# The last features of the second feed-forward product: as plain products in the slabs' seven banks instead of eight output tiles

## The chip, the core and the metric

The kernel runs on one core of a Trainium2 chip. It is one program for the whole two-layer trunk, launched once. The metric is device time in microseconds (us) of one execution, as the median of several runs; one more execution was recorded by the profiler, and everything that is said below about single instructions comes from that execution.

## The reference, cut to what matters

The trunk works on 256 tokens of width 2048 in float32. Layer 0 has a pooling mixer and memory attention, layer 1 differential and memory attention; each ends in the same feed-forward part:

```python
D_MODEL, SEQ, DEPTH, D_FF = 2048, 256, 2, 8192

def squared_relu_mlp(h, w1, w2):
    z = jax.nn.relu(h @ w1)
    return (z * z) @ w2

def reference(...):
    for i in range(DEPTH):
        ...                                   # attention or pooling, output projection
        x = x + squared_relu_mlp(rms_norm(x, ffn_norm[i]), w_ff1[i], w_ff2[i])
    return x
```

The change is in `(z * z) @ w2`, 8192 features to 2048 columns, in both layers. After layer 0's comes the projection of the shared keys and values; layer 1's is the last thing that the program does.

## The kernel before, in words

**Precision.** A float32 product is made of three passes in a rounded float32 format. Both factors are split into a high part (a cast) and a low part (value minus high part): for activations once, beforehand; for weights as they stream in. A weight goes from memory into `raw` (or `slab`, `room`), ScalarE casts it into a slot of `hi_ring` (line 195), and VectorE subtracts for `lo_ring` (line 198). The rings have six slots of 512 columns. `Feed.fill` prepares weights three jobs ahead of the job that TensorE is on (`AHEAD`), and not before slots are free. The load of a weight itself is issued further ahead, from SyncE.

**Tiles.** In a tile (`a_part`, lines 456 and 458) the weight block of 128 x 128 is the stationary side. A matmul against high and low part of the activations (512 columns) and one against the high part alone (256 columns) give 128 output columns for all tokens, transposed, as the residual `resid` is held. `c_tile` (lines 470 to 472) does the same in three matmuls of 256 columns.

**Slabs.** For most of the second product the weights are the moving side. A slab takes a pair of 128-feature blocks (256 features), both token halves, and two 512-column groups (one half `g` of the 2048 columns), as a 2 x 2 block product in the form with seven products in place of eight. Each of the seven has its own PSUM bank, p0 to p6, in which all slabs of the half add up. A product is three matmuls of 128 x 512 (`product`, lines 943, 945, 946). The seven are done as four jobs, with weights that are sums of the four weight blocks:

- job 0, the left blocks as loaded (1024 columns in `slab`), banks 0 and 1;
- job 1, the first 512 columns of `slab`, after a DMA from POOL (GpSimd) has added another weight block in place (`add_right`, line 170, issued after job 0's split), bank 2;
- job 2, the second weight row (`room`, 1024 columns), after VectorE added job 1's sum to it (line 224), banks 3 and 4;
- job 3, `room` again, after a second POOL DMA has added a block to it (issued after job 2's split) and VectorE one more (line 238), banks 6 and 5.

So within a slab there are four splits and two POOL DMAs in one chain. The jobs of neighbouring slabs overlap: slab p's jobs 1 and 2 come between job 0 of slab p+1 and job 3 of slab p-1.

**Order of the work.** Python code writes the instructions down in order; `at(n, ...)` puts a step n ticks later, `tick()` passes one. A scheduler then orders each engine's queue by its estimates. The 56 first-product tiles of a layer (`up_tile`) produce 64 blocks of features; 8 of these blocks come from a block product of the same kind ahead of them. A table of due times (`tiles_at`) spreads slab jobs between the tiles. The slabs of the halves alternate in groups of four pairs; at a change of half `swap` copies each bank out and `restore` (line 1093) copies the other half's back.

**The end of the product before.** Half 0 gets all 32 pairs as slabs, half 1 only the first 24, so there are 56 slabs. For the last 8 pairs (16 blocks of features), half 1's 1024 columns are done as eight tiles of 16 blocks, `down_tile(0)` to `down_tile(7)`. Twelve slab jobs of half 0 are left when they begin, two before each of tiles 0 to 5, and `finish_banks` closes half 0 within the last tiles: it adds up the banks (lines 1170 to 1174), scales rows, turns 128 x 128 pieces on TensorE (`turn`, line 1185) and adds them to `resid` (line 1186). Half 1's banks were closed earlier (`close_left`, `turn_left`, line 1146). In layer 1 tile 7 is a `c_tile`, over 12 blocks of `z` and then over 4 in `zr` that were scaled beforehand (line 901), so that after the last matmul one addition (line 915) and one output DMA (line 2049) remain. `done(n)` sends output column block n in layer 1, and prepares the next norm in layer 0.

Of the kernel before, what the change touches and what calls it, by code (L numbers as in the profile page):

```python
# [17 lines left out]
P = 128  # L18
# [8 lines left out]
PER_PART = 56  # L27
# [28 lines left out]
class Plan:  # L56
# [7 lines left out]
    def __init__(self):  # L64
        self.entries = []
        self.npos = 0
        self.jobs = []
        self.slabs = []

# [31 lines left out]
class Feed:  # L101
# [65 lines left out]
    def add_right(self, n, t):  # L167

        h = self.plan.row["S", n, 1]
        self.nc.gpsimd.dma_start(t, self.wst[h, :, 0:512], accum_op=ALU.add)  # L170
# [40 lines left out]
    def _prepare(self, p):  # L211
# [22 lines left out]
        if p[2] == 0:  # L234
            self.add_right(p[1], ra[:, 0:512])
        elif p[2] == 2:
            self.add_right(p[1], rb[:, 512:1024])
            add(rb[:, 0:512], rb[:, 0:512], ra[:, 512:1024])
# [35 lines left out]

    def used(self, n=1):
# [6 lines left out]
    def slab(self, rows):  # L282

        if self.dry:
            self.plan.slabs.append(rows)
        self.slab_no += 1
        return self.slab_no - 1
# [9 lines left out]
    def job_used(self, n, j):  # L297
        if not self.dry:
            self.free(("S", n, j))

# [11 lines left out]
def program(ctx, tc, plan, dry, xT, memT, par, lam, cst, wst, yT):  # L312
# [129 lines left out]
    def a_part(ps, w, l, n, ks, xs, first=True, last=True, between=None, rows=None):  # L442
# [4 lines left out]
        while i < len(ks):  # L447
# [7 lines left out]
            for c, k, hi, lo in two:  # L455
                nc.tensor.matmul(ps, hi, xs[:, k, :], start=first and c == 0, stop=False)  # L456
# [337 lines left out]
    def ffn(l, xs, tags, done, z, sums_in, f_place):  # L794
# [6 lines left out]

        room = sp.tile([P, 8192], F32, tag=tags[1], name=f"room{l}")
        staged = sp.tile([P, 2048], F32, tag="big2", name=f"stage{l}")
        sit = [sums_in[:, j, :] for j in range(4)]
        stage = [staged[:, T * j : T * j + T] for j in range(6)]
        sums = [room[:, 512 * j : 512 * j + 512] for j in range(2)]
        outs = [room[:, 1024 + 512 * j : 1536 + 512 * j] for j in range(2)]
# [19 lines left out]
        def evict(ps):  # L827
            x = outs[cnt[0] % 2]
            cnt[0] += 1
            return x, nc.scalar.copy(x, ps)  # L830
# [4 lines left out]
        def convert(j):  # L835
            a = stage[j % 6]
            k = j % NK

            def high():
                z_free[k] = False  # L840
                nc.scalar.copy(z[:, k, 0:T], a)
                at(1, low)

            def low():
                nc.vector.tensor_sub(z[:, k, T : 2 * T], a, z[:, k, 0:T].bitcast(F32))
# [3 lines left out]
            if j % 2 == 0:  # L849
                return  # L850
            i = j // 2

            def ready():
                return j in z_done and j - 1 in z_done and sit_free[i % 4]

            def combine():
                summed_up.add(i)
                sit_free[i % 4] = False
                a11, a21 = stage[2 * i % 6][:, 0:P], stage[2 * i % 6][:, P:T]
                a12, a22 = stage[(2 * i + 1) % 6][:, 0:P], stage[(2 * i + 1) % 6][:, P:T]  # L860
                s1, s2, s3, s4 = (sums[i % 2][:, c * P : c * P + P] for c in range(4))
                nc.vector.tensor_sub(s1, a21, a22)
                nc.vector.tensor_sub(s3, a11, a21)
                nc.vector.tensor_sub(s2, s1, a11)
                nc.vector.tensor_add(s4, a12, s2)
                at(1, sums_high)
                at(2, sums_low)

            def sums_high():
                nc.scalar.copy(sit[i % 4][:, 0:512], sums[i % 2])  # L870

            def sums_low():
                nc.vector.tensor_sub(
                    sit[i % 4][:, 512:1024], sums[i % 2], sit[i % 4][:, 0:512].bitcast(F32)
                )
                sit_done.add(i)

            when(ready, combine)

        def up_tile(i, ps, between=None):  # L880
# [5 lines left out]
            y, out = evict(ps)  # L886
            at(1, lambda: nc.vector.tensor_add(y[:, 0:T], y[:, 0:T], y[:, T : 2 * T]))
            at(2, lambda: nc.scalar.activation(y[:, 0:T], y[:, 0:T], AF.Relu))

            def square():  # L890
                assert i < 6 or i - 6 in z_done and (i - 6) // 2 in summed_up
                nc.scalar.activation(stage[i % 6], y[:, 0:T], AF.Square)
                at(1, lambda: convert(i))

            at(2, square, 2)

        scaled = []

        def scale_z(j):
            a, b = stage[j % 6], scaled[0][:, j % NK, :]  # L900
            one = nc.vector.tensor_mul(a, a, r[0])
            if not dry:
                feed.order(one, feed.last_cast.ins.name)
            split_plain(b, a)

        def down_tile(n, ps, between=None):
            ks = range(3 * NK, 4 * NK)
            if l == 1 and n == 7:
                c_tile(ps, "w_ff2", l, n, ks[:12], z, feat)
                x = outs[cnt[0] % 2]  # L910
                nc.vector.tensor_mul(x[:, 0:T], ps[:, 0:T], r[0])
                nc.vector.tensor_add(resid[:, n, :], resid[:, n, :], x[:, 0:T])
                ps = mmt("ff2")
                c_tile(ps, "w_ff2", l, n, ks[12:], scaled[0], feat)
                nc.vector.tensor_add(resid[:, n, :], resid[:, n, :], ps[:, 0:T])
                done(n)
                return
            if l == 1 and n == 6:
                scaled.append(sp.tile([P, NK, 512], F32R, tag="S0", name="zr"))
                for j in ks[12:]:  # L920
                    at(j - 59, lambda j=j: scale_z(j))
            a_part(ps, "w_ff2", l, n, ks, z, between=between, rows=feat)
            x, _ = evict(ps)

            def add():
                nc.vector.tensor_add(x[:, 0:T], x[:, 0:T], x[:, T : 2 * T])
                nc.vector.tensor_mul(x[:, 0:T], x[:, 0:T], r[0])
                nc.vector.tensor_add(resid[:, n, :], resid[:, n, :], x[:, 0:T])
                done(n)

            at(1, add)
# [16 lines left out]
        def slab_jobs(g, i, again, end):  # L948
# [4 lines left out]
                    [("w_ff2", l, feat[k], c, 4), ("w_ff2", l, feat[k + 1], c, 4)]  # L953
# [4 lines left out]
            def plain(c, t):  # L958
                assert k + c in z_done
                zk = z[:, (k + c) % NK, :]  # L960
                return zk[:, t * P : t * P + P], zk[:, T + t * P : T + t * P + P]
# [13 lines left out]
            def run(j):  # L975
                hi, lo = feed.job(n, j)
                for c, (p, a) in enumerate(sides[j]):
                    s = slice(512 * c, 512 * c + 512)
                    assert holds[p] == g
                    product(p, g, end, a(), hi[:, s], lo[:, s])  # L980
                feed.job_used(n, j)
                if j == 3 and not again:
                    sit_free[i % 4] = True
                    if i < 24:
                        z_free[k % NK] = z_free[(k + 1) % NK] = True

            return run

# [45 lines left out]
        def close_first(j):  # L1034
# [20 lines left out]
            for p in of_job[j]:  # L1055
                restore(p, 0)

        def turn_first(h):
# [7 lines left out]
            x, _ = evict(t4.rearrange("p c t -> p (c t)"))  # L1066
# [3 lines left out]

            def square():
                for k in (i, i + 1):
                    assert k < 6 or k - 6 in z_done and (k - 6) // 2 in summed_up
                nc.scalar.activation(staged[:, T * (i % 6) : T * (i % 6) + 512], x, AF.Square)
                at(1, lambda: convert(i))
# [1058 lines left out]
```

## Time and profile before

| | |
|---|---|
| median of 3 runs | 1983.58 us (1983.49 to 1983.89) |
| profiled execution: its span | 1982.8 us |
| TensorE (PE) busy | 1977.6 us |
| VectorE (DVE) busy | 1806.6 us |
| ScalarE (ACT) busy | 1571.6 us |
| GpSimd (POOL) busy | 239.3 us |
| layer 0's eight tiles end at | about 913 us |
| layer 1's last 56 tiles, slabs and eight tiles end at | about 1979 us |

The profiled execution has no time of its own beside its span: its span is 0.8 us under the median of the timed runs. In a row of the trace a time "907.88 0.62" is a start and a duration in us. A TensorE duration contains its pipeline's depth, so the rate is read from the starts of consecutive matmuls. In a row by shape, "x192 | 60.2, 395 | 0.0" means 192 instructions, 60.2 us busy, 395 ns each on average, and 0.0 us of idle time just before them. "PEld" is the load of the stationary side, SP is SyncE, and "SPq" and "POOLq" are the queues through which these engines issue DMAs.

### The profile page before, as it was taken

What the parts mean: (1) busy time and instruction counts of PE and PEld (TensorE: products, weight loads), DVE (VectorE), ACT (ScalarE), POOL (GpSimd) and SP (SyncE); (2) the same over time, 40 slices, a digit from 0 to 9 for tenths busy, and PEclk for the clock granted to TensorE, in tenths of its full rate; (3) what the DMA queues carried; (4) which work ended last, traced back from release to release, by engine and by line L of the source; (5) the groups of instructions that cost most, each with busy time, mean ns of one, the idle gap of its engine ahead of it and who ended that gap; (6) DMA issues with size and microseconds to landing.
All of it is one profiled execution on the core that took longest, in us unless ns stands there. A gap on an engine that the chain in (4) does not pass through costs nothing.

```text
span 1982.8 us, 31946 instructions
## 1 busy us (share of the span) xinstructions
PE 1977.6 (100%) x10356; PEld 1685.5 (85%) x10356; DVE 1806.6 (91%) x3313; ACT 1571.6 (79%) x2886; POOL 239.3 (12%) x281
## 2 busy tenths in 40 slices
PE   9999999999999999999999999999999999999999
PEld 7888888888888888888888889888888888888888
DVE  8898889999999999889989798989999999999888
ACT  7766677788878888778768799777788888888775
POOL 0000011111111111110110000001111111111110
PEclk9999999999999999999999999999999999999999
DMA  9556578888888888767886434568888888988874
GB/s 312 183 183 195 189 207 229 236 232 235 237 233 232 231 233 227 226 182 222 246 222 191 166 127 143 197 188 240 235 231 229 235 234 229 242 231 227 227 207 146
DMA packets 151080, 426.92 MB, mean 215 GB/s; under 512 B 17024, under 2 KB 19712, under 8 KB 150912
## 3 DMA queue, kind: packets, MB, share of 16 engines
q1 hardware_dynamic: 111024, 352.50, 53.2%
q0 software_dynamic: 39744, 72.37, 22.0%
q8 instruction: 81, 1.33, 0.3%
q14 instruction: 87, 0.71, 0.1%
q10 hardware_dynamic: 144, 0.01, 0.0%
HBM read 422.72 MB, written 2.10 MB: 214 GB/s over the span
## 4 chain that ended last, share of the span: by engine, by line
PE 99%; DMA 0%; ACT 0%; SPq 0%; issue 0%; DVE 0%; ACTq 0%
PE x_bank L456 22%; PE x_bank L458 11%; PE p L943 10%; PE p L945 10%; PE p L946 10%; PE wo L456 6%; PE wo L458 3%; PE u L456 2%; PE ff L456 1%; PE u L458 1%; PE q L490 1%; PE q L492 1%; PE q L491 1%; PE mk L492 1%; PE mk L490 1%; PE vp L1642 1%
## 5 line engine op out<-in xcount | busy, mean ns | idle before, releaser
L195 ACT CAST hi_ring<-raw 128x512 fp32r<-128x512 f32 x897 | 547.5, 620 | 167.3 <-PE x_bank L456 39.7
L198 DVE TENSOR_TENSOR lo_ring<-raw,hi_ring 128x512 fp32r<-128x512 f32 x897 | 605.1, 686 | 46.7 <-ACT hi_ring L195 39.9
L456 PE MATMUL x_bank<-fx,hi_ring 128*128 128x512 f32 x1728 | 540.1, 394 | 0.0
L458 PEld LDWEIGHTS x_bank<-fx,lo_ring 128*128 128x128 f32 x1728 | 324.5, 188 | 73.5
L198 DVE TENSOR_TENSOR lo_ring<-room,hi_ring 128x1024 fp32r<-128x1024 f32 x256 | 312.7, 1222 | 44.1 <-ACT hi_ring L195 42.5
L195 ACT CAST hi_ring<-room 128x1024 fp32r<-128x1024 f32 x256 | 269.8, 1054 | 94.4 <-PE x_bank L456 43.2
L458 PE MATMUL x_bank<-fx,lo_ring 128*128 128x256 f32 x1728 | 339.6, 278 | 0.0
L456 PEld LDWEIGHTS x_bank<-fx,hi_ring 128*128 128x128 f32 x1728 | 286.3, 189 | 26.0 <-ACT room L830 1.5
L198 DVE TENSOR_TENSOR lo_ring<-slab,hi_ring 128x1024 fp32r<-128x1024 f32 (+1 forms) x276 | 263.3, 954 | 33.3 <-ACT hi_ring L195 30.2
L195 ACT CAST hi_ring<-slab 128x1024 fp32r<-128x1024 f32 (+1 forms) x276 | 227.7, 834 | 52.5 <-PE p L945 28.2
L170 POOL DMA_DIRECT2D slab<-in_w x138 | 119.6, 866 | 1172.0 <-DVE lo_ring L198 854.0
L943 PE MATMUL p<-hi_ring,sit 128*128 128x512 f32 x480 | 188.3, 392 | 0.0
L945 PE MATMUL p<-hi_ring,sit 128*128 128x512 f32 x480 | 187.4, 390 | 0.0
L946 PE MATMUL p<-lo_ring,sit 128*128 128x512 f32 x480 | 186.6, 389 | 0.0
L170 POOL DMA_DIRECT2D room<-in_w x128 | 110.8, 866 | 486.5 <-DVE lo_ring L198 456.6
L456 PE MATMUL wo<-cat,hi_ring 128*128 128x512 f32 x512 | 161.6, 397 | 0.0
L943 PE MATMUL p<-hi_ring,z 128*128 128x512 f32 x368 | 145.2, 395 | 0.1
L945 PE MATMUL p<-hi_ring,z 128*128 128x512 f32 x368 | 143.9, 391 | 0.0
L946 PE MATMUL p<-lo_ring,z 128*128 128x512 f32 x368 | 143.4, 390 | 0.0
L458 PEld LDWEIGHTS wo<-cat,lo_ring 128*128 128x128 f32 x512 | 95.9, 188 | 22.3
L946 PEld LDWEIGHTS p<-lo_ring,sit 128*128 128x128 f32 x480 | 90.1, 188 | 19.7
L943 PEld LDWEIGHTS p<-hi_ring,sit 128*128 128x128 f32 x480 | 90.0, 187 | 13.1
(495 smaller groups left out, 3610.7 us busy)
## 6 DMA issues: line engine op xcount, KB each, us to landing
raw<-in_w SPq DMA_DIRECT2D x446, 512.0 KB, 4.3
slab<-in_w SPq DMA_DIRECT2D x138, 512.0 KB, 5.7
slab<-in_w POOLq DMA_DIRECT2D x138, 256.0 KB, 5.3
room<-in_w SPq DMA_DIRECT2D x128, 256.0 KB, 4.7
room<-in_w POOLq DMA_DIRECT2D x128, 256.0 KB, 5.5
resid<-in_x SPq DMA_DIRECT2D x8, 256.0 KB, 5.1
kv<-in_mem SPq DMA_DIRECT2D x8, 256.0 KB, 5.3
out_y<-resid SPq DMA_DIRECT2D x16, 128.0 KB, 1.9
```

Of the source, the lines that this page charges most:

```text
L170: self.nc.gpsimd.dma_start(t, self.wst[h, :, 0:512], accum_op=ALU.add)
L195: self.last_cast = self.nc.scalar.copy(hi, src)
L198: low = self.nc.vector.tensor_sub(lo, src, hi.bitcast(F32))
L456: nc.tensor.matmul(ps, hi, xs[:, k, :], start=first and c == 0, stop=False)
L458: nc.tensor.matmul(ps[:, T : 2 * T], lo, xs[:, k, 0:T], start=False, stop=last and c == len(ks) - 1,)
L490: nc.tensor.matmul(ps[t], x[t][1], hi, start=k == 0, stop=False)
L491: nc.tensor.matmul(ps[t], x[t][0], hi, start=False, stop=False)
L492: nc.tensor.matmul(ps[t], x[t][0], lo, start=False, stop=k == NK - 1)
L943: nc.tensor.matmul(ps, a[1], hi, start=new, stop=False, **again)
L945: nc.tensor.matmul(ps, a[0], hi, start=False, stop=False, **again)
L946: nc.tensor.matmul(ps, a[0], lo, start=False, stop=end, **again)
L1642: nc.tensor.matmul(bank, a[0], lo, start=False, stop=end)
```

## The change

There are no `down_tile`s any more. Both halves get 29 pairs as slabs in layer 0 (58 slabs) and 30 in layer 1 (60 slabs). The last 3 pairs (2 in layer 1) go feature by feature into the same banks: a 128 x 512 weight block (`quad`) is split plainly and used for two products, one for each token half, in banks 1 and 6 (first column group) or 4 and 2 (second). The order of these quads, of the last slab jobs, of the closing of single banks, of transposes and outputs is a table by hand per layer, `TAILS`: "A3010" is a plain quad of half 1 (A) or 0 (B), pair 30, block 1, column group 0; "581" is slab 58's job 1; "c1b3" closes bank 3 of half 1 as far as it can be; "h630" a quad whose weights are kept for two uses, here for bank 6; "t10st" a turn; "4@..." a step some ticks later.

```diff
+GROUPS = ((4, 4, 4, 4, 4, 4, 4, 1), (4, 4, 4, 4, 4, 4, 4, 2))
+BY_TWO = (False, True)
+TAILS = (
+    """
+    A2900 551 A2901 552 A2910 543 A2911 A3000 560 c1b0 A3001 553 A3100 A3101 c1c0
+    A3010 561 A3011 562 c1b3 A3110 A3111 c1c1 570 c0b0 563 c1b6 c1b5u c1b5t
+    571 B2910 B2900 B2901 572 c0b3 B3000 B3001 B2911 573 B3100 B3101 c0c0 c0b6
+    c0b5u B3010 B3011 t00st B3110 t01o B3111 1@d8 2@d9 3@d10 4@d11
+    1@c0c1 2@c0b5t 5@t10st 5@t11o 6@d12 6@d13 7@d14 7@d15
+    """,
+    """
+    A3000 561 A3001 562 A3010 553 A3011 570 c1b0 A3100 563 A3101 c1c0 571
+    A3110 572 c1b3 A3111 c1c1 580 573 c1b6 c1b5u c1b5t 581 B3010 582 B3011 590 c0b0 583 591 B3110
+    592 c0b3 B3111 c0c1 h630 593 h631 !c0b6 !c0b5u !c0b5t t10st h130 t11o h131 t01st last t00ta t00tb
+    """,
+)
...
+        def plain_quad(g, c, i, e):
+            hi, lo = feed.quad(weights(g, c, i, e))
+            for p in ((1, 6), (4, 2))[c]:
+                product(p, g, (i, e) == (31, 1), side(p, i, e), hi, lo)
+            feed.used(4)
...
+        def scaled_sum(s):
+            x = results[0]["c11"][:, s]
+            stt(x, banks[1][:, s], r[1][:, 0:1], x, ALU.mult, ALU.add)
...
+            elif what == "c1":
+                nc.scalar.copy(new("t"), banks[2])
+                sub(o["t"], o["t"], o["u"])
+                free(2)
+                add(new("c12"), o["t"], banks[4])
+                free(4)
+                scale_rows(o["c12"], 0)
...
-            x, _ = evict(t4.rearrange("p c t -> p (c t)"))
...
+            x = outs[h % len(outs)]
+            nc.scalar.copy(x, t4.rearrange("p c t -> p (c t)"))
+            to = resid[:, c : c + 2, :].rearrange("p c t -> p (c t)")
+            nc.gpsimd.dma_start(to, x, accum_op=ALU.add)
...
+        def turn(n, t, tag, cols=(0, 4)):
+            x = results[0][(("c11", "c12"), ("u6", "t"))[t][n]]
+            a, b = cols
+            t4 = pp.tile([P, 4, P], F32, tag=tag, bufs=1, name="ct")
+            for e in range(a, b):
+                nc.tensor.transpose(t4[:, e, :], x[:, e * P : e * P + P], ident)
+            at_c, at_t = slice(8 + 4 * n + a, 8 + 4 * n + b), slice(t * P, t * P + P)
+            nc.vector.tensor_add(resid[:, at_c, at_t], resid[:, at_c, at_t], t4[:, a:b, :])
+            if l == 1:
+                nc.sync.dma_start(yT[:, at_c, at_t], resid[:, at_c, at_t])
...
-            return 12.5 + 0.78 * (p - 4) if p <= 47 else 46.04 + 1.6 * (p - 47)
+            if p <= 41:
+                return 12.5 + 0.78 * (p - 4)
+            return 41.36 + 14.2 * (p - 41) / (w - 42)
...
-            while len(jobs) > 12:
+            while jobs:
...
-            for n in range(8):
-                if n < 6:
-                    some(ends[n][0])
-                if n == 5:
-                    finish_banks()
-                ps = bank() if n < 6 else mmt("ff2")
-                down_tile(n, ps, between(n) if n < 6 else None)
+            for x in order:
+                ...
+                if turns and x[0] in ("slab", "plain"):
+                    turn_left(turns.pop(0))
+                run(*x, now=soon)
+                if x[0] in ("slab", "plain") or x[0][0] == "h":
+                    tick()
```

`restore` after a bank's closing hands it to the other half at once. Half 1 is now the half that is closed first, inside the table, and its turned results go into `resid` in layer 1 by four POOL DMAs that add (`turn_left`, after.py line 1271); half 0 is closed at the end and turned by `turn`. In layer 1 two tiles' features are squared and converted at a time (`BY_TWO`), and the sums for a pair take three VectorE instructions in place of four.

Three places show the new order. The first is TensorE in layer 1, from job 2 of the last slab (bank p4 is its last) to job 3 of that slab (banks p6 and p5); `x_bank` is the bank of a `down_tile`. Before:

```order
L945 MATMUL p4_13146<-hi_ring_71,sit1_12278 128x512
L946 MATMUL p4_13146<-lo_ring_72,sit1_12278 128x512
L456 MATMUL x_bank_18758<-z1_12277,hi_ring_71 128x512 [waits Activation_49]
L456 MATMUL x_bank_18758<-z1_12277,hi_ring_71 128x512
L458 MATMUL x_bank_18758<-z1_12277,lo_ring_72 128x256 [waits DVE_49]
L458 MATMUL x_bank_18758<-z1_12277,lo_ring_72 128x256
L456 MATMUL x_bank_18758<-z1_12277,hi_ring_71 128x512 x2
L458 MATMUL x_bank_18758<-z1_12277,lo_ring_72 128x256 x2
```

After, from the second product of the quad "B3111" on, which follows job 2 of slab 59 at once:

```order
L1014 MATMUL p2_12945<-hi_ring_71,z1_12157 128x512
L1011 MATMUL p6_13023<-hi_ring_71,z1_12157 128x512 [waits Activation_49]
L1013 MATMUL p6_13023<-hi_ring_71,z1_12157 128x512
L1014 MATMUL p6_13023<-lo_ring_72,z1_12157 128x512 [waits DVE_49]
L1011 MATMUL p6_13023<-hi_ring_71,z1_12157 128x512 [waits Activation_49]
L1013 MATMUL p6_13023<-hi_ring_71,z1_12157 128x512
L1014 MATMUL p6_13023<-lo_ring_72,z1_12157 128x512 [waits DVE_49]
L1011 MATMUL p1_12944<-hi_ring_71,z1_12157 128x512
L1013 MATMUL p1_12944<-hi_ring_71,z1_12157 128x512
L1014 MATMUL p1_12944<-lo_ring_72,z1_12157 128x512
L1011 MATMUL p6_13023<-hi_ring_71,z1_12157 128x512 [waits Activation_49]
L1013 MATMUL p6_13023<-hi_ring_71,z1_12157 128x512
```

Before, the tile's 32 matmuls stand between the two jobs; now 15 matmuls do (two products of B3111, two for "h630", one for bank 1), and job 3 begins with the last two rows.

The second place is POOL's queue at the end of layer 1, where `slab` and `room` are the adds within slabs. Before:

```order
L170 DMA slab704_18325<-in_w 128x512 [waits DMAHW5_49,DMASW1_49,DVE_49]
L170 DMA room1_12988<-in_w 128x512 [waits DMAHW7_49,DMASW0_49,DVE_49]
L170 DMA slab710_18480<-in_w 128x512 [waits DMAHW2_49,DMASW3_49,DVE_49]
L170 DMA room1_12988<-in_w 128x512 [waits DMAHW3_49,DMASW2_49,DVE_49]
L170 DMA room1_12988<-in_w 128x512 [waits DMAHW0_49,DVE_49]
```

After:

```order
L186 DMA slab717_18313<-in_w 128x512 [waits DMASW5_49,DMAHW1_49,DMASW4_49,DVE_49]
L186 DMA room1_12868<-in_w 128x512 [waits DMAHW7_49,DVE_49]
L186 DMA slab720_18364<-in_w 128x512 [waits DMASW7_49,DMAHW6_49,DMASW6_49,DVE_49]
L1271 DMA resid_76<-room1_12868 128x512 [waits Activation_49]
L1271 DMA resid_76<-room1_12868 128x512 [waits DMASW0_49,Activation_49]
L1271 DMA resid_76<-room1_12868 128x512 [waits DMASW1_49,Activation_49]
L186 DMA room1_12868<-in_w 128x512 [waits DMAHW1_49,DMASW2_49,DVE_49]
L1271 DMA resid_76<-room1_12868 128x512 [waits DMASW3_49,Activation_49]
```

The last slab's add into `room` now stands behind three of the adds into `resid`, each of which waits for a copy by ScalarE.

The third place is the end of VectorE's queue; `ct` is a bank of transposes. Before:

```order
L1186 TENSOR_TENSOR resid_76<-resid_76,ct_18999 128x512 [waits PE_49]
L911 TENSOR_TENSOR room1_12988<-ff2_18960,r_x_13052 128x256 [waits PE_49]
L912 TENSOR_TENSOR resid_76<-resid_76,room1_12988 128x256 [waits DVE_49]
L915 TENSOR_TENSOR resid_76<-resid_76,ff2_19021 128x256 [waits DVE_49,PE_49]
L2114 UNCONDITIONAL_BRANCH
```

After:

```order
L1228 TENSOR_TENSOR keep_12871<-room1_12868,p6_13023 128x512 [waits PE_49]
L1282 TENSOR_TENSOR resid_76<-resid_76,ct_18580 128x4x128 [waits PE_49]
L1238 TENSOR_TENSOR keep_12871<-keep_12871,p5_13022 128x512 [waits DVE_49]
L1241 TENSOR_TENSOR keep_12870<-keep_12870,p5_13022 128x512
L402 SCALAR_TENSOR_TENSOR room1_12868<-p1_12944,d_x_13007,room1_12868 128x256 [waits PE_49]
L402 SCALAR_TENSOR_TENSOR room1_12868<-p1_12944,d_x_13007,room1_12868 128x256
L1282 TENSOR_TENSOR resid_76<-resid_76,ct_18606 128x4x128 [waits PE_49]
L1282 TENSOR_TENSOR resid_76<-resid_76,ct_18593 128x4x128 [waits PE_49]
L1282 TENSOR_TENSOR resid_76<-resid_76,ct_18615 128x2x128
L1282 TENSOR_TENSOR resid_76<-resid_76,ct_18620 128x2x128 [waits PE_49]
L2251 UNCONDITIONAL_BRANCH
```

Where one addition followed the last product, the closing of bank 5, the sum with bank 1 and five additions of turned pieces now stand around it. On TensorE twelve transposes, for the last four of these additions, come behind the last product.

More of the change, by code (lines that the diff above doesn't have):

```diff
@@ L273, in block, with held, release @@
         return hi[:, s], lo[:, s]
+    def held(self, what):
+        both = self.quad(what)
+        self.pos += 4
+        if self.dry:
+            self.plan.npos = self.pos
+        return both, self.pos // 4 - 1
+    def release(self, n):
+        if not self.dry:
+            self.free(("N", n))
     def used(self, n=1):
@@ L859, in combine @@
[L859 to L866, printed above, removed]
+                summed_up.add(m)
@@ L897, in ffn @@
[L897 to L916, printed above, removed]
-                return
[L918 to L931, printed above, removed]
@@ L1200, in tiles_at @@
+        slabs = []
+        for h, n in enumerate(groups):
+            first = sum(groups[:h])
+            g = (len(groups) - h) % 2
+            slabs += [(g, i, True) for i in range(first, first + n)]
+            slabs += [(1 - g, i, False) for i in range(first, first + n)]
+        n_slabs = len(slabs)
+        w = n_slabs - groups[-1] - 1
+        singles = range(left_pairs, 32)
         def tiles_at(p):
@@ L1271, in ffn @@
         due(56)
[L1272 removed]
         feed.loads_ahead = LOADS
[L1275 to L1277 removed]
         def last():
[L1280 to L1294 removed]
+            order = TAILS[l].split()
@@ new lines, in run @@
+            def run(what, *a, now=False):
+                if what == "slab":
+                    jobs[:] = [(0, *a)]
+                    one_job()
+                elif what == "plain":
+                    plain_quad(*a)
+                elif what[0] == "h":
+                    held(int(what[1]), int(what[2:]))
+                elif what[0] == "c":
+                    g, x = int(what[1]), what[2:]
+                    close(g, x) if now else at(1, lambda: close(g, x))
+                elif what == "last":
+                    scaled_sum(slice(0, T))
+                    scaled_sum(slice(T, 512))
+                elif what[0] == "t":
+                    n, t = int(what[1]), int(what[2])
+                    turn(n, t, what[3:].rstrip("ab"), {"a": (0, 2), "b": (2, 4)}.get(what[-1], (0, 4)))
+                elif what[0] == "d":
+                    done(int(what[1:]))
@@ new lines, in last @@
+            waited = 0
+            for x in order:
+                d, _, x = x.rpartition("@")
+                x = read(x.lstrip("!")) + (x[0] == "!",)
+                x, soon = x[:-1], x[-1]
+                if d:
+                    at(int(d), lambda x=x: run(*x, now=True))
+                    continue
+                while not can(*x):
+                    tick()
+                    waited += 1
+                    assert waited < 60, (l, x)
+                if turns and x[0] in ("slab", "plain"):
[3 more added lines that the diff above has]
+                    tick()
```

333 lines of the change are left out of this document (201 added, 132 removed).

## The prediction

> **What bounds the kernel now.** The page comes first: the span, the busy row, and the chain that ended last.
>
> ```profile
> span 1982.8 us, 31946 instructions
> ...
> PE 1977.6 (100%) x10356; PEld 1685.5 (85%) x10356; DVE 1806.6 (91%) x3313; ACT 1571.6 (79%) x2886; POOL 239.3 (12%) x281
> ...
> PE 99%; DMA 0%; ACT 0%; SPq 0%; issue 0%; DVE 0%; ACTq 0%
> ```
>
> TensorE is the whole chain. Its waits are the next view (engine, line, what it waited for, us, times, longest):
>
> ```profile
> PE warm L396 <- PEq L2107: 0.8, 1, 0.8
> PE mk L490 <- ACT hi_ring L195: 0.6, 1, 0.6
> PE mk L483 <- ACT hi_ring L195: 0.2, 1, 0.2
> ```
>
> They are 1.6 us in all and lie at the start. So every microsecond of matmuls taken away is won, as long as the new order still feeds TensorE. How near the others are is shown by a stretch with tiles and slabs (first row) and by the end (second row): busy time of PE, PEld, DVE, ACT, POOL, then granted clock, DMA share, GB/s.
>
> ```profile
> 1720.00:1820.00 100.00, 100.00 (x506) 84.44 (x504) 95.21 (x147) 85.29 (x142) 19.04 (x22) 1.00 0.87 233
> 1900.00:1983.00 83.00, 79.36 (x450) 69.11 (x448) 69.52 (x122) 50.86 (x86) 6.05 (x7) 0.99 0.57 165
> ```
>
> In the end stretch there is throughput to spare: DVE is busy 69.5 us of 83, ACT 50.9. What the change can lose there is latency, which averages don't show, so I followed single chains.
>
> **Matmuls removed and added.** The rate is read from starts: tile blocks in layer 0's last tile, a turn's transposes, products, and the last `c_tile`; then the tiles' counts.
>
> ```profile
> 907.88 0.62 PE L456 MATMUL ff<-z,hi_ring 128*128 128x512 f32 x2
> ...
> 913.46 0.27 PE L1185 MATMUL ct<-const,c_b 128*128 128x128 f32 x1
> 913.57 0.27 PE L1185 MATMUL ct<-const,c_a 128*128 128x128 f32 x1
> ...
> 1959.66 0.39 PE L946 MATMUL p<-lo_ring,z 128*128 128x512 f32 x1
> ...
> 1960.34 0.39 PE L946 MATMUL p<-lo_ring,sit 128*128 128x512 f32 x1
> ...
> 1972.70 0.28 PE L471 MATMUL ff<-z,hi_ring 128*128 128x256 f32 x1
> ...
> 1975.34 0.28 PE L472 MATMUL ff<-z,lo_ring 128*128 128x256 f32 x1
> ```
> ```profile
> L456 PE MATMUL x_bank<-z,hi_ring 128*128 128x512 f32 x192 | 60.2, 395 | 0.0
> L456 PE MATMUL ff<-z,hi_ring 128*128 128x512 f32 x48 | 15.2, 398 | 0.0
> ```
>
> A block of a tile (one matmul of each width): 913.46 - 907.88 is eight pairs of blocks, so 0.349 us a block. A product's matmul: 0.68 / 3 = 0.2275. A `c_tile` matmul: 2.64 / 22 = 0.12.
>
> Removed: 192 + 48 = 240 blocks x 0.349 = 83.7; layer 1's tile 7, 16 blocks x 3 x 0.12 = 5.8; together 89.5 us.
> Added: in layer 0 two slabs (14 products) and 3 pairs x 2 blocks x 2 column groups x 2 halves = 24 quads of two products (48); in layer 1 four slabs (28) and 16 quads (32). That is 122 products of three matmuls: 366 x 0.2275 = 83.3 us.
> TensorE saves **6.2 us**. Twelve transposes moved behind the last product take another 12 x 0.11 = **1.3 us** from what is ahead of it.
>
> Cheaper at no time of its own: layer 1's conversions by two, three VectorE instructions for four in the sums, and fewer tile evictions. TensorE hides them all, since it waits for nothing there. The slab pace from p = 41 on is no denser than the stretch shown, so I cost it at nothing; the price if its cover went is whatever VectorE's 4.8 idle us in 100 don't hold.
>
> **What was behind the tiles.** With the tiles gone between a slab's jobs, the chain inside a slab can come to light. Its parts, by shape and from the last slabs:
>
> ```profile
> L195 ACT CAST hi_ring<-room 128x1024 fp32r<-128x1024 f32 x256 | 269.8, 1054 | 94.4 <-PE x_bank L456 43.2 <-PE p L945 27.8 <-PE p L946 6.8
> L195 ACT CAST hi_ring<-raw 128x512 fp32r<-128x512 f32 x897 | 547.5, 620 | 167.3 <-PE x_bank L456 39.7 <-PE wo L456 38.1 <-PE u L456 17.4
> L198 DVE TENSOR_TENSOR lo_ring<-room,hi_ring 128x1024 fp32r<-128x1024 f32 x256 | 312.7, 1222 | 44.1 <-ACT hi_ring L195 42.5
> L198 DVE TENSOR_TENSOR lo_ring<-raw,hi_ring 128x512 fp32r<-128x512 f32 x897 | 605.1, 686 | 46.7 <-ACT hi_ring L195 39.9 <-PE p L945 2.8 <-PE u L456 0.7
> L224 DVE TENSOR_TENSOR room<-slab,room 128x512 f32<-128x512 f32 x128 | 87.7, 685 | 0.0
> L830 ACT COPY room<-x_bank 128x512 f32<-128x512 f32 x136 | 79.1, 582 | 15.8 <-PE x_bank L458 14.4 <-PE x_bank L1146 1.4
> L1093 ACT COPY p<-room 128x512 f32<-128x512 f32 x46 | 27.0, 591 | 1.7 <-DVE stage L1122 1.0 <-DVE room L1125 0.2
> ```
> ```profile
> 1937.43 1.23 DVE L198 TENSOR_TENSOR lo_ring<-room,hi_ring 128x1024 fp32r<-128x1024 f32 x1
> 1938.95 0.86 POOL L170 DMA_DIRECT2D room<-in_w  x1 [6.75 <-DVE lo_ring L198]
> 1963.32 0.72 ACT L1137 ACTIVATE c_a<-c_a,d_x 128x512 f32<-128x512 f32 x1 [0.77 <-DVE c_a L1173]
> 1965.60 0.42 DVE L901 TENSOR_TENSOR stage<-stage,r_x 128x256 f32<-128x256 f32 x1
> 1966.05 0.41 ACT L438 CAST zr<-stage 128x256 fp32r<-128x256 f32 x1 [0.30 <-DVE stage L901]
> 1966.54 0.42 DVE L439 TENSOR_TENSOR zr<-stage,zr 128x256 fp32r<-128x256 f32 x1
> ```
>
> From an end to the next start: VectorE to POOL 1938.95 - 1938.66 = 0.29, VectorE to ScalarE 0.03, ScalarE to VectorE 0.08. The time from a POOL DMA's issue to its landing: the medians of the last 83 us, then least, median and greatest of `room` from 1880 and of `slab` from 1800 on:
>
> ```profile
> room<-in_w POOLq DMA_DIRECT2D x4, 256.0 KB, 4.9
> slab<-in_w POOLq DMA_DIRECT2D x3, 256.0 KB, 3.9
> ```
> ```profile
> DMA to landing us min/median/max: 3.2/3.9/6.0
> ```
> ```profile
> DMA to landing us min/median/max: 3.7/5.3/7.8
> ```
>
> Layer 1, slab 58 ("580" to "583" of the table). Time 0 is the matmul of job "571" that sets two slots free. Job 0's cast and subtraction end at 0.2 + 1.05 + 0.08 + 1.22 = 2.6; the POOL DMA is issued at 2.9 and lands 3.9 later, 6.8. The sum into `room` ends at 7.6, job 2's cast at 8.7. VectorE then has two additions of the closing and a 512-wide subtraction until 9.6 (the closing's additions stand ahead of weights in its queue), and job 2's subtraction ends at 10.8. POOL issues at 11.1, and 4.9 later, at 16.0, the second add is in; job 3's cast ends at 17.15, and TensorE can begin "583" at 17.25. Until then it has 58 matmuls, 58 x 0.2275 + 0.11 = 13.3. It waits **4.0 us**.
>
> Right behind, ScalarE is late: cast 0.6, scale 0.72, bank copy 0.6, scale 0.72 and copy of turned pieces 0.58 come to 3.2 before the second group of half 1's transposes, against 2.4 of TensorE work, and job "591"'s cast after them: 0.8 + 0.2 = **1.0 us**. Before job "592" a copy, a scale from PSUM and a 1.05 cast follow each other: **1.1 us**.
>
> Slab 59, the last, counted from the same time 0: job 2's subtraction ends at 25.2. In POOL's queue three adds into `resid`, the third behind ScalarE's copy, stand ahead of the add into `room`, which is issued at 25.66 and lands 4.9 later, at 30.56; with the cast of 1.05 and the handoffs "593" can begin at 31.8. Ahead of it TensorE has 15 matmuls and two of job 2, 17 x 0.2275 = 3.9 (before, the tile alone was 16 x 0.349 = 5.6), and is there at 29.2: **2.6 us**. Layer 1's waits: 8.7 us.
>
> Layer 0, slab 57: cast and subtraction end at 3.0, POOL at 3.3, landing 7.2, cast 0.62, and then ScalarE puts a bank copy of 0.6 ahead of TensorE's start at 8.6; there are 31 matmuls, 7.05. That is 1.55, and with a ScalarE queue of 4.3 against 3.5 of TensorE before "572" another 0.8: **2.4 us**. Other work follows layer 0, so its end costs nothing.
>
> Hidden: SyncE issues six `room` and six `slab` loads more and twelve `raw` loads fewer, ahead of need as now, with the DMA share at 0.57 in that stretch; without that cover, one landing, about the 4 us shown. The adds into `resid` come well before their output; the price of POOL's place is in slab 59's chain.
>
> **The end.** Now:
>
> ```profile
> 1979.08 0.28 PE L472 MATMUL ff<-zr,lo_ring 128*128 128x256 f32 x1
> ...
> 1979.39 0.42 DVE L915 TENSOR_TENSOR resid<-resid,ff 128x256 f32<-128x256 f32 x1 [0.55 <-PE ff L472]
> ```
>
> The last matmul is through at 1979.08 + 0.12 = 1979.20, VectorE starts 0.19 later and ends at 1979.81, and the output's way takes 2.99 to 1982.8: 3.6 us. After: counted from the last product, VectorE is still at bank 5 (bank 6's addition waited for bank 6, 1.8 us earlier), and ends the two 512-wide operations at 1.0, the scaled sums (two of 0.42) at 1.9, three additions of 512 or 256 at 3.6. The last transposes wait for the bank of the ones before them: 3.9, the last addition 4.5, the output 7.5. The end is **3.9 us** longer.
>
> **The sum.** -6.2 - 1.3 + 8.7 + 2.4 + 3.9 = +7.5 us on the span of 1982.8: 1990.3. The median of the timed runs is 0.8 over that span, so **1991.1 us**.
>
> A fixed price can be set against these landings. The Trainium skill, "DMA: Bandwidth & Descriptors", section "Anatomy of one DMA — SWDGE (gpsimd) path", gives about 2.0 us plus the bytes over 436 thousand per us for such a DMA. For 262144 bytes that is 2.6 us, an estimate from that page. The rows above are longer, 3.9 and 4.9, in a stretch where other transfers run. By the page's figure the four landings would take 7.2 us from the waits, and the sum would be +0.3.
>
> Bounds. With landings at the least rows (3.7 and 3.2) the four waits on them lose 0.4 + 3.4 = 3.8: +3.7. With 5.3 and 6.0 they gain 2 x 1.4 + 2 x 1.1 = 5.0: +12.5, or 1996.1. I take the medians of the end stretch, since they lie nearest in time. ScalarE's queue terms (1.0, 1.1, 0.8) could vanish if the estimates of the end of casts are late: with the least landings too, +0.8.
>
> **The rivals.** 0.2%, or 4 us, is about what a measurement of this kernel can tell from no change.
>
> 1. The weights arrive anyway. Preparation runs three jobs ahead, and if the casts come earlier than slots suggest, no wait shows: -7.5 + 3.9 = -3.6, 1980.0 us, within 0.2%. For it: 1.6 us of waits in all now, with DVE at 95%. Against it: slots are freed by the very matmuls between which the chain lies.
> 2. The other side: the waits are hidden and VectorE is done with bank 5 while the last quad runs, so that the end stays 3.6 us: -7.5, 1976.1 us, faster. It decides once waits and the longer end together are under 3.5 us. Against it is the order of VectorE's last ten instructions, five of which need banks that are complete only at the end.
> 3. Quick landings, as a kernel whose loads are nearly over could have: the least rows give +3.7, 1987.3 us, within 0.2%. For it, the 3.2 row; against it, 4.9 in the very stretch.
> 4. The clock drops after the long waits. After the start's wait, TensorE's matmuls were long, where 395 ns is usual:
>
> ```profile
> L483 PE MATMUL mk<-hi_ring,mems 128*128 128x512 f32 x4 | 1.9, 572 | 0.2 <-ACT hi_ring L195 0.2
> ```
>
> Ten such matmuls behind each of the two long waits cost 20 x 0.18 = 3.6: 1994.7 us. The Trainium skill, "TensorE: Matmul & The Clock Gate", section "HAM oscillation — how this bites in real kernels", says TensorE should not idle over about 3.4 us, or it is throttled. The granted clock of 0.99 in the end stretch shows nothing of this, since it has no such gap.
>
> **How the numbers follow.** Chances: the forecast 0.60 (0.05 of it in its lowest part, under +4 us), the first rival 0.13, the second 0.15, the third 0.05, the fourth 0.07. Faster 0.15; within 0.2% 0.13 + 0.05 + 0.05 = 0.23; slower 0.55 + 0.07 = 0.62. The range reaches from the first rival, 1979.5, to the upper landings, 1996.5, and leaves out the second rival and some of the fourth.
>
> **What would show it.** Right: 366 more product matmuls and none of tiles from `z`; in the waits of PE, rows of products on `hi_ring` of 2 us and more in all of 11, in the last 35 us of layer 1 and around 900 us in layer 0; about 7.5 us from the last product to the end. Wrong: no such rows, or POOL's last adds issued much earlier than the casts they wait for here. If TensorE's products came slower than 0.2275, or VectorE filled up earlier in the layers, the first terms would be wrong.

## The result, and the profile after

The changed kernel takes 2002.43 us (median of 4 runs, 1998.91 to 2005.16), the kernel before 1983.6: a ratio of 1.0095 (95% interval 1.0083 to 1.0107). It is slower by about 18.8 us, where 7.5 were forecast and the range ended at 1996.5. The profiled execution has a span of 1998.7, 15.9 over the one before, so the working below is against 15.9. Two things make the 2.9 between these numbers: the execution profiled after was 1.9 under its median (2000.55 of 2002.43), and in all timed runs of the experiments and of the changed kernel the time lies 1.7 to 2.3 us over the span, so a span of 1982.8 belongs to an execution about 1 us slower than the usual one before. In this comparison the runs before lie within 0.4 us of each other, these within 6.

```profile
PE 1979.0 (99%) x10194; PEld 1674.0 (84%) x10194; DVE 1782.5 (89%) x3133; ACT 1570.2 (79%) x2831; POOL 252.6 (13%) x297
```

TensorE's waits, which were 1.6 us in three rows, all at the start (rows of the start and some short ones are left out here):

```profile
PE p L1011 <- ACT hi_ring L211: 4.4, 3, 2.8
PE kp L1777 <- ACT hi_ring L211: 2.3, 1, 2.3
PE ct L1280 <- DVE resid L1282: 1.2, 1, 1.2
PE vp L1779 <- DVE lo_ring L214: 1.1, 2, 0.7
PE tc_x L601 <- DVE acc L1476: 1.1, 1, 1.1
PE ct L1280 <- ACT keep L1249: 1.0, 1, 1.0
...
PE x_bank L1259 <- DVE resid L1264: 0.7, 1, 0.7
```

Rows of `p`, `x_bank` and `ct` are in the tails, where I had looked. `kp` and `vp` are not: they belong to the projection of shared keys and values, behind layer 0, as `tc_x` belongs to the norm there. A wait in this view counts from the modelled end of the pipeline, so a gap between starts is longer than its row by about 0.16 us. The stretches that answer to those shown of before (busy time of PE, PEld, DVE, ACT, POOL, then granted clock, DMA share, GB/s):

```profile
1728.00:1828.00 100.00, 100.00 (x510) 85.01 (x509) 89.76 (x126) 84.16 (x133) 18.14 (x21) 1.00 0.87 234
1915.00:1998.70 83.70, 72.49 (x334) 56.41 (x332) 63.39 (x92) 52.86 (x82) 12.44 (x15) 0.97 0.64 165
```

The layers' body is as full as before, with VectorE at 90% instead of 95. In the end stretch TensorE is busy 87% of the time instead of 96 and VectorE 76 instead of 84, while ScalarE is at 63 instead of 61 and POOL at 15 instead of 7. No engine is full there, so what is lost is latency, and some of it goes with a clock of 0.97.

Where the time comes in, by the start of the same instruction in both traces:

| instruction | before | after | difference |
|---|---|---|---|
| first matmul of `v<-hi_ring,x_kv` (behind layer 0) | 943.07 | 944.52 | +1.45 |
| first of `kp<-hi_ring,x_kv` | 1004.20 | 1007.13 | +2.93 |
| last of `kp<-lo_ring,kv_sums` | 1056.37 | 1064.05 | +7.68 |
| last of `wo<-cat,hi_ring`, ahead of layer 1's feed-forward part | 1309.55 | 1317.19 | +7.64 |
| end of the span | 1982.8 | 1998.7 | +15.9 |

The first matmul of `wo` stands at 159.69 before and 158.96 after. All kernels of the study that have any of the new order have it between 158.4 and 159.5, whatever their tails, and it lies ahead of all that the change is about, so these 0.7 us are put down to chance. Against them layer 0 and the projection behind it cost 8.4 us, layer 1's feed-forward part another 8.3.

### The profile page after: what moved, and what is told of

It is laid out like the page before. It is cut to its first block, busy times and chain, and to the rows that moved or that the text cites. A ratio compares the mean times of both kernels' runs of the same rounds, so it can differ in the third digit from the quotient of the medians.

```text
span 1998.7 us, 31468 instructions
## 1 busy us (share of the span) xinstructions
PE 1979.0 (99%) x10194; PEld 1674.0 (84%) x10194; DVE 1782.5 (89%) x3133; ACT 1570.2 (79%) x2831; POOL 252.6 (13%) x297
## 5 line engine op out<-in xcount | busy, mean ns | idle before, releaser
L211 ACT CAST hi_ring<-raw 128x512 fp32r<-128x512 f32 x873 | 533.4, 619 | 155.4 <-PE wo L510 37.8
L214 DVE TENSOR_TENSOR lo_ring<-raw,hi_ring 128x512 fp32r<-128x512 f32 x873 | 590.4, 686 | 45.3 <-ACT hi_ring L211 41.6
L214 DVE TENSOR_TENSOR lo_ring<-room,hi_ring 128x1024 fp32r<-128x1024 f32 x268 | 327.4, 1223 | 72.7 <-ACT hi_ring L211 66.7
L211 ACT CAST hi_ring<-room 128x1024 fp32r<-128x1024 f32 x268 | 282.1, 1053 | 127.0 <-PE p L1013 49.4
L214 DVE TENSOR_TENSOR lo_ring<-slab,hi_ring 128x1024 fp32r<-128x1024 f32 (+1 forms) x288 | 274.8, 954 | 36.5 <-ACT hi_ring L211 33.0
L211 ACT CAST hi_ring<-slab 128x1024 fp32r<-128x1024 f32 (+1 forms) x288 | 237.6, 834 | 56.4 <-PE p L1013 30.2
L1011 PE MATMUL p<-hi_ring,sit 128*128 128x512 f32 x524 | 206.3, 394 | 0.9 <-ACT p L1180 0.6
L1013 PE MATMUL p<-hi_ring,sit 128*128 128x512 f32 x524 | 205.1, 391 | 0.0
L1014 PE MATMUL p<-lo_ring,sit 128*128 128x512 f32 x524 | 204.4, 391 | 0.0
L1011 PE MATMUL p<-hi_ring,z 128*128 128x512 f32 x446 | 176.1, 395 | 4.2 <-ACT hi_ring L211 4.2
L1014 PE MATMUL p<-lo_ring,z 128*128 128x512 f32 x446 | 174.2, 392 | 0.7 <-DVE lo_ring L214 0.7
L1013 PE MATMUL p<-hi_ring,z 128*128 128x512 f32 x446 | 174.9, 392 | 0.0
```

Source lines behind the costliest of these rows:

```text
L211: self.last_cast = self.nc.scalar.copy(hi, src)
L214: low = self.nc.vector.tensor_sub(lo, src, hi.bitcast(F32))
L1011: nc.tensor.matmul(ps, a[1], hi, start=new, stop=False, **again)
L1013: nc.tensor.matmul(ps, a[0], hi, start=False, stop=False, **again)
L1014: nc.tensor.matmul(ps, a[0], lo, start=False, stop=end, **again)
```

## The experiments

**Which half.** In the first kernel layer 0 has its eight tiles and layer 1 the new order; the second has it the other way round. Both call the function `ffn` of before for one layer:

```diff
-    down = ffn(0, fx, ...)
+    down = ffn_tiles(0, fx, ...)      # ffn of before; in the second kernel for layer 1
```

> Layer 0 ends with its eight tiles as before, layer 1 with the new order. Theory A (the loss has two halves: layer 0's end reaches into the projection of keys and values, 7.7 + 0.7 = 8.4 us, and layer 1's tail costs the other 8.3): span 1982.8 + 8 = about 1991, and no wait of TensorE in the projection (kp, vp). Theory B (the waits in the projection are a chance collision of loads, whatever layer 0 does): about 1991 to 1996, with waits in kp or vp in some profile.

> Layer 0 in the new order, layer 1 with its eight tiles as before. Theory A: about 1991, the same 1.5 us in vp and 4.7 us in kp, and nothing at the end. Theory B: between 1983 and 1991, with other waits in the projection than in the kernel after.

The new order in layer 1 alone: 1991.48 us, ratio 1.0041 (1.0026 to 1.0056), +8.4. In layer 0 alone: 1993.62, 1.0052 (1.0037 to 1.0067), +10.5. The two add up to the whole; the second is 2.6 above the 1991 that was expected, and its four runs lie 5 us apart. The first has no wait of TensorE in the projection, the second has them at the same places as the changed kernel.

**Is it the turn of buffers?** The change shifts which of three buffers a slab's second row goes to in the projection.

```diff
-    feed.second = [kv[:, 3072:4096], kv2[:, 0:1024], kv2[:, 1024:2048]]
+    feed.second = [kv2[:, 0:1024], kv2[:, 1024:2048], kv[:, 3072:4096]]
```

> The kernel after, with the three buffers for second weight rows in the projection of keys and values handed out in the turn that they had before (the slab count of layer 0 went from 64 to 66 with the first product's eight, so the turn by the number modulo 3 was shifted by two). Theory C (the shifted turn of buffers makes the loads late): the 4.7 us in kp go, total about 4 to 5 us under the kernel after. Theory A (VectorE comes late out of layer 0): within 1 us of the kernel after.

> The kernel after once more, for a second profile and its spread on this chip. Theory A: the same places wait (vp, kp, the products before 583 and 593, the two last turns), each within 0.5 us. Theory B: the waits in kp differ by microseconds from run to run.

2000.92 us with the buffers turned back (+17.8), 2002.26 (+19.2) for the changed kernel on the same chip: no difference outside the intervals, and the `kp` wait is there (2.39 us). Theory C falls. The second profile of the changed kernel waits at the same places with other lengths: 1.42 for 2.29 at `kp`, 2.21 for 0.70 at the transposes of layer 0. That is more than the 0.5 us which theory A allowed, and less than the microseconds at `kp` of theory B: the places repeat, the lengths don't.

**One cast in front of two.** In the changed kernel's trace ScalarE's row that waited longest there, the two behind it, the issue of the load that it waited for, and TensorE:

```profile
1026.05 0.90 SPq L172 DMA_DIRECT2D raw<-in_w  x2
```
```profile
1035.98 0.62 ACT L211 CAST hi_ring<-raw 128x512 fp32r<-128x512 f32 x1 [4.68 <-DMA raw<-in_w]
1036.51 1.04 ACT L211 CAST hi_ring<-kv 128x1024 fp32r<-128x1024 f32 x1
1037.45 1.04 ACT L211 CAST hi_ring<-slab 128x1024 fp32r<-128x1024 f32 x1
```
```profile
1037.60 0.50 PE L1777 MATMUL kp<-hi_ring,x_kv 128*128 128x512 f32 x1 [2.29 <-ACT hi_ring L211]
```

ScalarE stood for 4.68 us on a load that took about nine, while the weights that TensorE needed next lay behind. In the order in which the weights are prepared, which the next kernel keeps, the cast of `slab` comes right behind that of `kv`, and the `raw` cast only behind two copies and two casts of `vv` that follow; here it stands two rows ahead of the slab's. The change lies some 100 us earlier; what it moved here is the scheduler's choice. The experiment holds casts to the order of preparation, in the projection only.

```diff
+        if self.in_turn and self.turn_cast is not None:
+            self.order(self.last_cast, self.turn_cast.ins.name)
+        self.turn_cast = self.last_cast
```

> The kernel after, with ScalarE's casts in the projection of keys and values held to the order in which the weights are prepared. In the kernel after the cast of one block, whose load had been issued at 1026.5 us and landed near 1035, stands ahead of two casts that were ready. Theory D (that one cast holds ScalarE, and TensorE behind it): the waits in kp of 1.5 to 2.5 and 0.7 us go, with the slow stretch behind them: 2.2 to 4.7 us less, near 1998. Rival (the load is late for TensorE too): the wait only moves to that block's own matmuls, total within 1 us of after.

1997.45 us, 1.0071 (1.0056 to 1.0086): +14.4, which is 4.8 less than the +19.2 of the changed kernel run again (each against the kernel before on its own chip). No row of `kp` is left among its waits; the longest are:

```profile
PE p L1014 <- ACT hi_ring L211: 5.1, 4, 2.3
PE x_bank L1262 <- DVE resid L1267: 1.9, 1, 1.9
```

**The landings in layer 1.** These kernels leave out the POOL adds of the last two, then of the last three slabs, so a part of the product is not computed.

```diff
-            self.add_block(p[1], 1, 0, ra[:, 0:512])
+            if p[1] < len(self.plan.slabs) - 2:          # then - 3
+                self.add_block(p[1], 1, 0, ra[:, 0:512])
...                                                       # the second add likewise
```

> The kernel after without the four POOL DMAs that add weights in the last two slabs of layer 1 (those slabs then use unsummed weights, so that part of the product is left out). Theory E (the landing of these adds is what TensorE waits for before jobs 583 and 593): both waits go, 2.7 and 2.5 to 2.9 us, and the slow stretches behind them: 5 to 7 us less, 1995 to 1997. Rival F (slots and the queues of ScalarE and VectorE are late anyway): 2 us less at most.

> As the kernel without POOL adds in the last two slabs of layer 1, but in the last three (57, 58, 59; that part of the product is left out). In that kernel a wait of 1.7 and 0.7 us stayed, before job 573 of slab 57. Theory E (landings of adds): it goes too, with the slow stretch behind it: 2.5 to 4 us less than with two slabs, near 1993 to 1994. Rival F (ScalarE and VectorE are late there by the closing of banks): the wait stays within 1 us.

Two slabs: 1997.2 us (+14.1; 1.0064, 1.0047 to 1.0081). The wait before 593 is gone, and one of 1.5 us stays before 573. Three slabs: 1992.97 (+9.8; 1.0049, 1.0034 to 1.0064), and it goes too. With three, what is left of TensorE's waits is layer 0's and the last turns':

```profile
PE x_bank L1261 <- DVE resid L1266: 2.2, 1, 2.2
PE vp L1781 <- DVE lo_ring L214: 1.4, 3, 0.7
PE ct L1282 <- DVE resid L1284: 1.4, 1, 1.4
PE kp L1779 <- ACT hi_ring L211: 1.3, 1, 1.3
```

So both waits for `p`, before 573 and 593, are waits for landings, and with what follows them they are worth about 9 us in the medians. Theory E holds, rival F falls. With three slabs the trace also shows what is left of the saving: from the last row of `wo` (1321.53) to the end of the last product (1986.19) it takes 664.7 us, before the change to the end of the last matmul 669.7. That is 5.0 less, where matmuls and moved transposes of layer 1 were to give 3.8 + 1.3.

**POOL's adds into `resid`.** They are made by VectorE here.

```diff
-            nc.gpsimd.dma_start(to, x, accum_op=ALU.add)
+            nc.vector.tensor_add(to, to, x)
```

> The kernel after with the four POOL DMAs into resid of layer 1 replaced by additions on VectorE. Theory G (those DMAs lie in the way of the last slab's add, which took 5.7 us to land against 4.4 for slab 58's): the wait before 593 is 1.0 to 1.5 us shorter, total 1 us less. Rival (its landing is as long without them, and VectorE has 2.4 us more to do): the same or up to 1 us more.

The last add into `room` and the cast that waits for it, in the changed kernel and here:

```profile
1978.52 0.98 POOL L186 DMA_DIRECT2D room<-in_w  x1
...
1984.25 1.04 ACT L211 CAST hi_ring<-room 128x1024 fp32r<-128x1024 f32 x1 [2.81 <-DMA room<-in_w]
```
```profile
1980.66 0.86 POOL L186 DMA_DIRECT2D room<-in_w  x1 [8.35 <-DVE lo_ring L214]
...
1985.41 1.04 ACT L211 CAST hi_ring<-room 128x1024 fp32r<-128x1024 f32 x1 [1.85 <-DMA room<-in_w]
```

5.73 us from issue to cast with them, 4.75 without: theory G is right on the landing, though its size varies: six other profiles with these adds have 5.1 to 5.5. But the total is 2001.82 (+18.8, against +19.2), no difference outside the interval: `ct` waits 2.1 us for VectorE where it waited 1.2.

**Layer 0's own tail.** In the first of three kernels ScalarE copies turned pieces out of their bank (against the changed kernel); the second is new layer 0, old layer 1, with casts in turn; the third adds turns at every second place, and "B2900" ahead of "571".

```diff
-                nc.vector.tensor_add(resid[:, c : c + 2, :], resid[:, c : c + 2, :], t4)
+                x = evict(t4.rearrange("p c t -> p (c t)"), 2 + h % 2)     # first; add later
...
-    571 B2910 B2900 B2901 572 c0b3
+    B2900 571 B2910 B2901 572 c0b3                                        # third
...
+                    skip[0] = l == 0 and not skip[0]                        # third
+                    if not skip[0]:
+                        turn_left(turns.pop(0))
```

> The kernel after with layer 0's turned pieces of half 1 copied out of their one bank by ScalarE, as before the change, and added from there, where after adds from the bank by VectorE. Theory H (the second turn waits for VectorE to come round to the first one's addition): the wait of the transposes, 0.7 to 2.4 us near 908, goes, and the total falls by as much. Rival: VectorE is as late at the next step, and the time comes back in the norm (tc_x) or in vp.

> New order in layer 0, the eight tiles in layer 1, and the casts of the projection held to the order of preparation. Theory A with D: of layer 0's share of 8 to 10 us the waits in kp and the slow stretch go (3 to 5 us), and about 5 us over the kernel before stay, 1988. If layer 0's own tail cost nothing, as the prediction had it, the time would be 1981 to 1984.

> As the kernel with old layer 1 and casts in turn, and in layer 0 the four turns of half 1 stand behind every second job or quad in place of every one, and one quad moves ahead of job 571. Theory H (turns come faster than VectorE can take the one bank): the wait of 2 us in the transposes goes and 0.7 before 571 too: 1985 to 1986. Rival (VectorE's work is only put off): tc_x and vp wait 1 to 2 us more, total as without.

First: 2000.9 us (+17.9), about one less than the changed kernel, within the intervals; the transposes wait 1.1 us for the copy instead. Second: 1988.13 (+5.0; 1.0025, 1.0015 to 1.0034). Third: 1988.21 (+5.0), no gain. The waits of the second and the third show why:

```profile
PE x_bank L1262 <- DVE resid L1267: 1.9, 1, 1.9
PE vp L2287 <- DVE lo_ring L217: 1.2, 3, 0.6
PE tc_x L604 <- DVE acc L1984: 0.9, 1, 0.9
...
PE p L1014 <- ACT p L1183: 0.6, 1, 0.6
```
```profile
PE p L1017 <- DVE lo_ring L217: 1.6, 3, 1.1
PE vp L2290 <- DVE lo_ring L217: 1.1, 2, 0.6
PE tc_x L604 <- DVE acc L1987: 0.8, 1, 0.8
PE x_bank L1262 <- DVE resid L1267: 0.8, 1, 0.8
```

The wait goes from the transposes to weights: all but one of these rows end on VectorE. Of theory H's rival the total holds, but not the place: `tc_x` and `vp` wait no longer than without, and products (`p`) wait 1.6 us for the low parts of weights. The kernel before already had VectorE nearly full here:

```profile
900.00:920.00 20.00, 20.00 (x119) 17.55 (x119) 19.58 (x42) 15.89 (x31) 0.00 (x0) 1.00 0.69 226
920.00:945.00 25.00, 25.00 (x116) 20.78 (x115) 24.07 (x56) 21.34 (x46) 0.00 (x0) 1.00 0.71 224
945.00:985.00 40.00, 39.98 (x176) 32.46 (x175) 38.28 (x68) 31.89 (x55) 6.92 (x8) 1.00 0.81 244
```

That is 96% for 85 us in which TensorE lost nothing, so there is little room to catch up. That the wait comes back for this reason is argued, not shown: no run here takes work off VectorE in this stretch, and it isn't fuller after the change (94% from 920 to 985 us in the second kernel).

**All of it.** New order in both layers, casts in turn, the third kernel's layer 0, and in layer 1 more quads ahead of 573 and 593:

```diff
-    A3011 570 c1b0 A3100 563 A3101 c1c0 571 A3110 572 c1b3 A3111 c1c1 580 573 ...
+    A3011 570 c1b0 A3100 563 571 572 A3101 c1c0 c1b3 A3110 A3111 c1c1 580 573 ...
-    h630 593 h631 ... t10st h130 t11o h131
+    h630 h130 593 h631 ... t10st t11o h131
```

> The new order in both layers with what the runs point to: casts in turn, turns apart, a quad ahead of 571, and in layer 1 more quads between jobs 572 and 573 (24 matmuls for 12) and one more ahead of 593. Theory: 3 to 4 us less before 573, 0.7 before 593, and layer 0 as in the kernel before this one: 1991 to 1993. Rival (the wait moves to job 571 or 572, which now come sooner): 1994 to 1996.

1997.28 us (+14.1; 1.0071, 1.0054 to 1.0088), as with the casts alone. The wait before 573 is gone, but others stand in its place: 0.8 us before 571, 0.3 and 0.5 at 572, and 2.4 in slab 58's jobs behind 573. The wait moved, as the rival said, but for the most part elsewhere, and the total lies above both ranges. No kernel of the study beats the one before.

## Why the prediction was wrong

**The step that failed** is in the sum for layer 0: "Other work follows layer 0, so its end costs nothing." The forecast for layer 0 was -2.4 of matmuls and 2.4 of waits, nothing in all; alone it costs 10.5 us. Of these about 5 are the displaced cast and the slow stretch behind it (the experiments with casts in turn), and 5.0 stay. In the trace of the kernel with these 5.0, 4.0 of the 4.6 us of waits behind the program's start are for VectorE; that they can't be made up because VectorE was at 96% there before is the likely reason, not a tested one. Only the two waits around job 571 had been forecast (0.4 and 0.7 us in starts for 1.55).

**The missing cover** behind it: how near the other engines are was read from a stretch in layer 1's body, where VectorE is busy 95.21 us of 100, and from the end; the stretch behind layer 0's tail was not read, and no cover is named for it. And an order written anew at one place was taken to leave the order elsewhere alone. The displaced cast stands in the changed kernel's queue some 100 us behind the last line that the diff touches.

**Layer 1** was right in sum, but not in its places: 7.5 forecast, 8.3 in the profile, 8.4 alone. Among the waits of products on `hi_ring`, of which 11 us were to be seen in both layers, the view has 4.4. In detail, with starts in the changed kernel's trace:

```profile
1959.05 0.39 PE L1014 MATMUL p<-lo_ring,z 128*128 128x512 f32 x1
1960.85 0.50 PE L1011 MATMUL p<-hi_ring,z 128*128 128x512 f32 x1 [1.42 <-ACT hi_ring L211]
...
1962.11 0.50 PE L1014 MATMUL p<-lo_ring,z 128*128 128x512 f32 x1 [0.53 <-DVE lo_ring L214]
...
1963.55 0.79 PE L1011 MATMUL p<-hi_ring,sit 128*128 128x512 f32 x1 [0.24 <-ACT hi_ring L211]
...
1965.54 0.63 PE L1013 MATMUL p<-hi_ring,z 128*128 128x512 f32 x1
1965.97 0.63 PE L1014 MATMUL p<-lo_ring,z 128*128 128x512 f32 x1
...
1982.19 0.39 PE L1014 MATMUL p<-lo_ring,z 128*128 128x512 f32 x1
1985.35 0.50 PE L1011 MATMUL p<-hi_ring,z 128*128 128x512 f32 x1 [2.77 <-ACT hi_ring L211]
...
1990.47 0.39 PE L1014 MATMUL p<-lo_ring,z 128*128 128x512 f32 x1
```

- The wait of 2.6 before 593 is there: 1985.35 - 1982.19 - 0.23 = 2.9.
- The wait of 4.0 before 583 isn't. The one slab earlier, before 573, has 1.57 + 0.69 + 0.41 = 2.7 between starts and a slow stretch of 1.5 behind it. Job 573 lies between 571, the forecast's time 0, and 583, so these 4.2 us gave slab 58's chain the time that it was to lack:

```profile
1970.16 1.05 ACT L211 CAST hi_ring<-room 128x1024 fp32r<-128x1024 f32 x1 [1.53 <-DMA room<-in_w]
```
```profile
1971.38 0.40 PE L1011 MATMUL p<-hi_ring,z 128*128 128x512 f32 x1
```

The cast for 583 waits for its landing as forecast and ends at 1971.21, and TensorE begins 583 at 1971.38 without a wait. What the forecast lacked is the same chain one slab earlier. What TensorE loses before 573 it no longer loses before 583, so the sum held; for a forecast without a term for 573 that is luck.

- ScalarE's terms, 1.0 and 1.1, came to 1.2 in small steps between 583 and 593 (10.81 us for 35 matmuls and 15 transposes, 7.96 + 1.65). Another 0.8 of such steps, not forecast, stands ahead of 573.
- The end is 1998.7 - 1990.70 = 8.0 from the last product, for 7.5.

The books of the profiled execution, the losses by subtraction from the table of starts: -0.7 at the start, -7.5 of matmuls, 4.6 up to the first `v`, 1.5 from there to `kp`, 4.7 from there to layer 1's feed-forward part, 9.0 in layer 1 ahead of the last product, and 4.4 of longer end make the 15.9, but for rounding. Of the 9.0 the terms above place 2.7 + 1.5 + 2.9 + 1.2 + 0.8 = 9.1. The products are as forecast: 366 more matmuls, and no tile from `z`. So the saving of 6.2 + 1.3 is there, as the kernel without three slabs' adds shows for layer 1, and buried.

**The rivals.** The first two (hidden waits) are refuted by the waits, quick landings by the medians of the last 59 us, which are those that the sum had taken (3.9 and 4.9):

```profile
room<-in_w POOLq DMA_DIRECT2D x4, 256.0 KB, 4.8
...
slab<-in_w POOLq DMA_DIRECT2D x3, 256.0 KB, 3.9
```

The fourth, the clock, occurred beside the forecast, and in smaller pieces: the last section. It was to follow the two long waits; in this trace it followed the wait before 573 and the one in `kp`, not the longest, before 593.

## What to carry to other kernels

A saving on the engine that bounds the kernel can be lost in stretches where the others have little to spare, also behind the edited code: read their busy share in each stretch there, not in the body alone. Set a chain at every slab of the new order, and let a wait that one has caused count as time for the next. Where a scheduler orders in-order queues by estimates, compare the order of the engines far behind the edit too, and look for an instruction that waits for a transfer ahead of some that are ready; here one such cast was worth 4.8 us, and a few lines that held the order won them back. Loosening one wait moved it to other places in three kernels here, with no gain.

## What the runs showed of the hardware

Behind a wait TensorE sometimes goes at about half its rate for some 3 us: in the rows above product matmuls come 0.43 us apart (1965.54 to 1965.97) where 0.2275 is usual, six to nine of them in a row, which costs 1.2 to 1.7 us. It followed waits of 1.3 to 2.4 us in some executions and not in others at the same place: behind 593 in the second profile of the changed kernel (2.32 us) but not in the first (2.77). With casts in turn three waits of 1.9 to 2.3 us had none behind them in the profile. What decides it isn't shown. Windows of the changed kernel's trace that hold such a stretch or a part of one show a granted clock below 1: 0.95 from 1020 to 1040 us, 0.97 from 1915 to the end. The spread of this kernel goes with it: of its four runs that of 1998.91 us has a clock of 0.999 over the whole, that of 2000.55 has 0.998, and those of 2004.32 and 2005.16 have 0.997. The Trainium skill, "TensorE: Matmul & The Clock Gate", section "HAM oscillation — how this bites in real kernels", sets idle gaps above about 3.4 us as what to avoid. No single gap between starts in these stretches was that long (3.16 us at most, and without a slow stretch behind it), so for this kernel the measurement decides: half rate followed a wait of 1.4 us with shorter ones behind it.
